# Attention of a streaming Conformer encoder: scores kept negated with a minimum, probabilities scaled by ScalarE, two score tiles of block 0 in one pair of banks

## The chip, the cores and the metric

The kernel runs on one core of a Trainium2 chip. The metric is the device time of one execution in microseconds, the median of several runs. Times within the execution are read from the profile of a single execution, counted from the start of its span. The engines are TensorE (PE in the profile; PEld is its weight load), VectorE (DVE), ScalarE (ACT), GpSimd (POOL) and SyncE (SP, which here issues nearly all DMAs, in order).

## The reference

One layer of a hybrid streaming encoder is computed in fp32 for a prompt of 2048 tokens and a sample chunk of 64 tokens, with model width 1024: a norm, one input projection into the parts of a convolution branch, q, k, v and two gates, then the convolution and the attention, a gated merge with an output projection, and a gated feed-forward part. The attention is over a band: 8 heads of 64 channels, where each chunk of 64 tokens reads its own chunk and the eight before it, with a bias by relative distance.

```python
    s = jnp.einsum('bqhd,bkhd->bhqk', q, k).astype(jnp.float32) * ATTN_SCALE
    rel = jnp.clip(q_pos[:, None] - k_pos[None, :], -MAX_REL, MAX_REL) + MAX_REL
    s = s + rel_bias[:, rel].astype(jnp.float32)[None]
    ...
    p = jax.nn.softmax(s, axis=-1).astype(v.dtype)
    return jnp.einsum('bhqk,bkhd->bqhd', p, v)
```

The attention is computed for the prompt's tokens and for the sample chunk, which reads 256 cached keys and its own 64.

## The kernel before, in words

Products of the big matrices are done in fp32 by pairs of a high and a low part (`whi`, `wlo`, `hh`, `hl`), three matmuls to a product, with their sums (`ps`) in PSUM. The first phase ends at about 1225 us of the profiled execution. It goes through the tokens in four blocks (0 to 576 with the sample chunk, then three of 512); the code numbers them 0 to 3, and the short name of the change calls block 0 block one. For each block the columns of the input projection are done in a fixed order of stages, q, k, v, gates and the two halves of the convolution's input. The norm of the next block's x tiles, the attention, the convolution's 31 taps (`y<-u,wd,y` on DVE, one instruction of 512 or 606 columns for each tap) and the output stages are generators that go alongside these products. They are called lanes. The class `Stream` keeps a modelled load for each engine, adds to it for every instruction, and pumps a lane on when the time or the room that it yielded is reached (`SCORE_ROOM`: DVE at most 2500 ns ahead of PE; `PE_LAG` is 400 ns). So the order of all instructions is fixed when the kernel is built, by these modelled loads and by the framework's own scheduler, and a changed instruction can move others far from it.

Attention works on heads, in block 0 alternately a prompt head and a sample head. A prompt head of block 0 has four score tiles of 128 tokens with 128, 256, 384 and 512 keys, a sample head one tile of 64 x 320, and a head of blocks 1 to 3 four tiles of 128 x 640, kept as twice 320 columns in two banks: 136 tiles in all. `attend` (L1397) writes a tile's scores with `pe.matmul` into `sc`, a pair of PSUM banks of which there is only one (pool `ps_a`, tag "s"), so that the next scores wait until the score pass has read the last. For each tile `softmax_max` (L1299) runs the score pass on DVE (`CUSTOM_DVE_ANT_0 pr<-sc,bias` in the profile, with a read of its accumulator behind it; `ISA pr,sm<-sc,bias` in the order of instructions): it scales scores plus bias into `pr` in SBUF and leaves the row's maximum in `sm`. DVE then negates the maximum (`TENSOR_SCALAR sm<-sm`), ACT takes the exponential with it as bias, and sums the row. `softmax_scale` takes the reciprocal of the sum on DVE and scales the probabilities, on DVE (`TENSOR_SCALAR pr<-pr,sm`) in blocks 0 to 2 and on ACT in block 3 (`ON_ACT`, L48). It is called for a tile after the next tile's scores. PE then transposes the probabilities (`ptp<-ident,pr`), ACT and DVE split them (`ph`, `pl`), and PE multiplies them with v (`po`).

In the profile nearly all engine instructions have one line, L104, that of a helper which records each operation; SP's loads have their own: L1085 x tiles (`x_t`), L1328 and L1329 q and k of a head, L1335 and L1337 its v, L486 stores and L456 loads of split weights, L1260 stores of the convolution's rows (`c_d`). In the changed kernel these lines are one or two off (L103, L1084, L1326, and so on).

Of the kernel before, what the change touches and what calls it, by code (L numbers as in the profile page):

```python
# [8 lines left out]
F32 = mybir.dt.float32  # L9
F32R = mybir.dt.float32r  # L10
AF = mybir.ActivationFunctionType
ALU = mybir.AluOpType
# [4 lines left out]
P = 128  # L17
# [26 lines left out]
PE_LAG = 400.0  # L44
# [3 lines left out]
ON_ACT = (3,)  # L48
# [9 lines left out]
SCORE_ROOM = {"dve": 2500}  # L58
# [530 lines left out]
def streaming_layer(ctx: ExitStack, tc: tile.TileContext, I, O):  # L589
    nc = tc.nc  # L590
    stream = Stream()
# [594 lines left out]

    def convolve(u, y, ct, b):
        w = UW if b == 0 else HIST + QB
        n = w - HIST
# [109 lines left out]
    def softmax_max(ps, n, w, bias):  # L1299
        pr = wk.tile([P, 640], F32, tag="pr", name="pr", bufs=8)  # L1300
        sm = wk.tile([P, 4], F32, tag="sm", name="sm", bufs=9)
        nb = ps.shape[1]
        stream.after("dve", "pe")
        dve.tensor_tensor_reduce(
            out=pr[:n, :w].rearrange("p (a b) -> p a b", a=nb), in0=ps, in1=bias.rearrange("p (a b) -> p a b", a=nb),
            scale=0.125, scalar=-3e38, op0=ALU.add, op1=ALU.max, accum_out=sm[:n, 0:1],
        )
        dve.tensor_scalar(sm[:n, 1:2], sm[:n, 0:1], -1.0, None, ALU.mult)
        free = stream.when("dve")
        stream.after("act", "dve")  # L1310
        act.activation(pr[:n, :w], pr[:n, :w], AF.Exp, bias=sm[:n, 1:2], accum_out=sm[:n, 2:3])
        return pr, sm, free, stream.when("act")

    def softmax_scale(pr, sm, n, w, on_act):
        dve.reciprocal(sm[:n, 3:4], sm[:n, 2:3])
        if on_act:
            stream.after("act", "dve")
            act.activation(pr[:n, :w], pr[:n, :w], AF.Copy, scale=sm[:n, 3:4])
        else:
            dve.tensor_scalar(pr[:n, :w], pr[:n, :w], sm[:n, 3:4], None, ALU.mult)  # L1320
# [57 lines left out]
    order, loaded, now = [], {}, {"scored": -1, "finished": -1, "bias": None}  # L1378
# [21 lines left out]
    def attend(i):  # L1400
# [8 lines left out]
        for t in range(0, nq, P):  # L1409
            n = min(P, nq - t)  # L1410
            ps = ps_a.tile([P, 2, 512], F32, tag="s", name="sc")
# [12 lines left out]
            if t + P < nq:  # L1424
                yield free + PE_LAG, SCORE_ROOM
            else:
                fetch(i + 1)
                now["scored"] = i
            if t:
                softmax_scale(*tiles[-2], x in ON_ACT)  # L1430
        yield ready
        softmax_scale(*tiles[-1], x in ON_ACT)
        yield stream.when("act" if x in ON_ACT else "dve") + PE_LAG
# [680 lines left out]
```

## Time and profile before

| | before |
|---|---|
| time, median of 3 runs (lowest to highest) | 3046.8 us (3046.7 to 3047.27) |
| the profiled execution | 3042.59 us |
| its span | 3040.8 us |
| mean granted clock of PE | 0.986 |
| PE busy | 2934.8 us, 97% of the span |
| DVE busy | 2052.4 us, 67% |
| ACT busy | 1256.8 us, 41% |
| POOL busy | 985.3 us, 32% |

Busy time is the time in which an engine ran at least one instruction. The granted clock is the share of TensorE's full rate that the throttle let through. A row of the timeline has a start, a length, the engine, the operation with its tiles (out<-in), and in brackets how long the engine had been idle before it and whose work ended that. Where a row says x6, it holds six instructions in succession.

### The profile page before, as it was taken

How to read it: one execution, taken by the hardware profiler on the slowest of the kernel's cores; microseconds unless marked ns; L12 is line 12 of the kernel's file. 1: busy time of each engine (PE TensorE's matmuls, PEld its weight loads, DVE VectorE, ACT ScalarE, POOL GpSimd, SP SyncE). 2: the span in 40 equal slices, each digit the busy share in tenths (PEclk: the TensorE clock that was granted, in tenths of full speed). 3: DMA queues.
4: the chain of work that ended last, by engine and by line, in shares of the span. 5: the costliest groups of instructions: out<-in, count | busy, mean ns of one | idle time of the engine just before them, and what ended most of it. 6: DMA issues, size and time to landing. Idle time of an engine off the chain costs nothing. (4 is left out here: it accounts for less than half of the span.)

```text
span 3040.8 us, 44889 instructions
## 1 busy us (share of the span) xinstructions
PE 2934.8 (97%) x16259; PEld 2606.5 (86%) x16259; DVE 2052.4 (67%) x3835; ACT 1256.8 (41%) x2267; POOL 985.3 (32%) x617
## 2 busy tenths in 40 slices
PE   7989898999999999989999999999999999999998
PEld 4889776888888788878989889999999898999997
DVE  5896678777977895467666755655666756366567
ACT  3324532453254257464444425534444244333332
POOL 1200120101011102355677433247767341333331
PEclk9999998999999999999999999999999999999999
DMA  9888788888997788886444786455556965355554
GB/s 305 268 275 299 230 286 278 275 263 268 305 284 243 247 265 282 253 285 215 149 143 144 231 290 207 157 165 190 182 194 201 342 215 190 118 167 173 166 160 176
DMA packets 487019, 690.98 MB, mean 227 GB/s; under 512 B 38420, under 2 KB 316808, under 8 KB 486797
## 3 DMA queue, kind: packets, MB, share of 16 engines
q1 hardware_dynamic: 474517, 670.72, 67.3%
q10 hardware_dynamic: 12280, 17.39, 1.6%
q8 instruction: 128, 2.10, 0.3%
q14 instruction: 94, 0.77, 0.1%
HBM read 503.79 MB, written 184.19 MB: 226 GB/s over the span
## 5 line engine op out<-in xcount | busy, mean ns | idle before, releaser
L104 POOL TENSOR_TENSOR wlo<-wst,whi 128x1024 fp32r<-128x1024 f32 (+1 forms) x180 | 401.4, 2236 | 491.6 <-ACT whi L104 463.9
L104 PE MATMUL ps<-t,whi 128*128 128x384 f32 (+1 forms) x2112 | 506.1, 324 | 10.0 <-DVE t L104 4.8
L104 PE MATMUL pd<-whi,hid 128*128 128x512 f32 (+1 forms) x1400 | 450.2, 391 | 3.4 <-DVE acc L104 3.4
L104 ACT ACTIVATE whi<-wst 128x1024 fp32r<-128x1024 f32 (+1 forms) x273 | 266.1, 979 | 358.6 <-PE ps L104 123.7
L104 PE MATMUL ps<-b,whi 128*128 128x384 f32 (+1 forms) x1584 | 381.7, 326 | 11.0 <-DVE pw L104 4.0
L104 PEld LDWEIGHTS ps<-t,whi 128*128 128x128 f32 x2112 | 370.7, 189 | 18.4 <-DVE t L104 5.9
L104 DVE SCALAR_TENSOR_TENSOR y<-u,wd,y 128x512 f32<-128x512 f32 (+1 forms) x480 | 369.3, 772 | 6.7
L104 PE MATMUL ps<-hh,whi 128*128 128x512 f32 (+2 forms) x992 | 364.6, 367 | 0.7 <-DVE h L104 0.7
L104 PE MATMUL ps<-hl,whi 128*128 128x512 f32 (+2 forms) x992 | 348.1, 351 | 0.0
L104 PE MATMUL ps<-hh,wlo 128*128 128x512 f32 (+2 forms) x992 | 347.6, 350 | 0.0
L104 DVE TENSOR_TENSOR acc<-acc,pd 128x512 f32<-128x512 f32 (+1 forms) x440 | 290.7, 684 | 80.5 <-PE pd L104 76.9
L104 PE MATMUL ps<-t,wlo 128*128 128x384 f32 (+1 forms) x1056 | 340.8, 323 | 0.0
L104 PEld LDWEIGHTS pd<-whi,hid 128*128 128x128 f32 (+1 forms) x1400 | 258.1, 184 | 64.7 <-DVE acc L104 6.9
L104 PEld LDWEIGHTS ps<-b,whi 128*128 128x128 f32 x1584 | 278.7, 190 | 14.3 <-DVE pw L104 4.3
L104 PE MATMUL pd<-wlo,hid 128*128 128x512 f32 (+1 forms) x700 | 273.7, 391 | 0.0
L104 PE MATMUL ps<-b,wlo 128*128 128x384 f32 (+1 forms) x792 | 257.3, 325 | 0.0
L104 POOL TENSOR_TENSOR r<-t,mhalf 128x8 f32<-128x8 f32 (+3 forms) x68 | 84.4, 1243 | 390.0 <-DVE t L104 380.1
L104 PEld LDWEIGHTS ps<-hh,wlo 128*128 128x128 f32 x992 | 188.6, 190 | 22.7
L104 POOL TENSOR_TENSOR wlo<-wup,whi 128x1024 fp32r<-128x1024 f32 (+1 forms) x64 | 138.2, 2160 | 213.0 <-ACT whi L104 190.7
L104 PEld LDWEIGHTS ps<-hh,whi 128*128 128x128 f32 x992 | 189.3, 191 | 19.7 <-issue 1.9
L104 PEld LDWEIGHTS ps<-hl,whi 128*128 128x128 f32 x992 | 189.3, 191 | 15.5 <-issue 1.4
L104 PEld LDWEIGHTS ps<-t,wlo 128*128 128x128 f32 x1056 | 199.3, 189 | 0.6
(217 smaller groups left out, 5717.5 us busy)
## 6 DMA issues: line engine op xcount, KB each, us to landing
whi<-w_din_h SPq DMA_DIRECT2D x72, 512.0 KB, 5.8
wlo<-w_din_l SPq DMA_DIRECT2D x72, 512.0 KB, 7.0
wst<-sum_d SPq DMA_DIRECT2D x131, 256.0 KB, 2.9
wmod<-in_w_ada SPq DMA_DIRECT2D x48, 512.0 KB, 6.7
sum_d<-ws SPq DMA_DIRECT2D x88, 256.0 KB, 3.2
wst<-in_w_ffn_in SPq DMA_DIRECT2D x85, 256.0 KB, 3.4
wst<-in_w_in SPq DMA_DIRECT2D x40, 512.0 KB, 7.1
wst<-in_w_ffn_in SPq DMA_DIRECT2D x37, 512.0 KB, 5.3
```

What stands on the lines that cost most here:

```text
L104: return f(*args, **kw)
```

## The change

The score pass multiplies by −0.125 and keeps a minimum, so that `pr` holds the negated scores and `sm` the negated maximum; the exponential takes it as bias with scale −1, and the negate on DVE goes. All probabilities are scaled on ACT. In block 0 the tiles of 128 and 256 keys are written into the two halves of one pair of banks, those of 384 and 512 into those of the next, and after the first of such two tiles the lane asks only for room, not for the modelled time at which the score pass frees the bank. The dictionary `now` is set up earlier and is given the score pass's instruction, which is not read.

```diff
@@ -45,7 +45,6 @@
 TURN_LAG = 2500.0
 KN_LAG = 5000.0
 X_LAG = 8000.0
-ON_ACT = (3,)
 ON_POOL = ()
 DMA_LAG = 4000.0
 OUT_LAG = 4000.0
@@ -1183,6 +1182,8 @@
                     )
         W.done()
         return u
+
+    now = {"scored": -1, "finished": -1, "bias": None}
 
     def convolve(u, y, ct, b):
         w = UW if b == 0 else HIST + QB
@@ -1298,26 +1299,23 @@
 
     def softmax_max(ps, n, w, bias):
         pr = wk.tile([P, 640], F32, tag="pr", name="pr", bufs=8)
-        sm = wk.tile([P, 4], F32, tag="sm", name="sm", bufs=9)
+        sm = wk.tile([P, 3], F32, tag="sm", name="sm", bufs=9)
         nb = ps.shape[1]
         stream.after("dve", "pe")
-        dve.tensor_tensor_reduce(
+        now["least"] = dve.tensor_tensor_reduce(
             out=pr[:n, :w].rearrange("p (a b) -> p a b", a=nb), in0=ps, in1=bias.rearrange("p (a b) -> p a b", a=nb),
-            scale=0.125, scalar=-3e38, op0=ALU.add, op1=ALU.max, accum_out=sm[:n, 0:1],
+            scale=-0.125, scalar=3e38, op0=ALU.add, op1=ALU.min, accum_out=sm[:n, 0:1],
         )
-        dve.tensor_scalar(sm[:n, 1:2], sm[:n, 0:1], -1.0, None, ALU.mult)
         free = stream.when("dve")
         stream.after("act", "dve")
-        act.activation(pr[:n, :w], pr[:n, :w], AF.Exp, bias=sm[:n, 1:2], accum_out=sm[:n, 2:3])
+        act.activation(pr[:n, :w], pr[:n, :w], AF.Exp, bias=sm[:n, 0:1], scale=-1.0, accum_out=sm[:n, 1:2])
         return pr, sm, free, stream.when("act")
 
-    def softmax_scale(pr, sm, n, w, on_act):
-        dve.reciprocal(sm[:n, 3:4], sm[:n, 2:3])
-        if on_act:
-            stream.after("act", "dve")
-            act.activation(pr[:n, :w], pr[:n, :w], AF.Copy, scale=sm[:n, 3:4])
-        else:
-            dve.tensor_scalar(pr[:n, :w], pr[:n, :w], sm[:n, 3:4], None, ALU.mult)
+    def softmax_scale(pr, sm, n, w):
+        stream.after("dve", "act")
+        dve.reciprocal(sm[:n, 2:3], sm[:n, 1:2])
+        stream.after("act", "dve")
+        act.activation(pr[:n, :w], pr[:n, :w], AF.Copy, scale=sm[:n, 2:3])
 
     def load_qk(h, q0, nq, k0, nk):
         hp, i = divmod(h, 2)
@@ -1375,7 +1373,7 @@
             )
         return bias
 
-    order, loaded, now = [], {}, {"scored": -1, "finished": -1, "bias": None}
+    order, loaded = [], {}
 
     def attention(b):
 
@@ -1408,7 +1406,9 @@
         tiles = []
         for t in range(0, nq, P):
             n = min(P, nq - t)
-            ps = ps_a.tile([P, 2, 512], F32, tag="s", name="sc")
+            if x != 0 or t % (2 * P) == 0:
+                both = ps_a.tile([P, 2, 512], F32, tag="s", name="sc")
+            ps = both if x != 0 or t % (2 * P) == 0 else both[:, 1:]
             if x not in (0, "s"):
                 for j in range(2):
                     for d in range(2):
@@ -1421,16 +1421,18 @@
                 src, bs = ps[:n, 0:1, :w], bias[:n, 64:384][:, ::-1] if x == "s" else bias[:, :w][:, ::-1]
             pr, sm, free, ready = softmax_max(src, n, w, bs)
             tiles.append((pr, sm, n, w))
-            if t + P < nq:
+            if x == 0 and t % (2 * P) == 0:
+                yield stream.load["pe"], SCORE_ROOM
+            elif t + P < nq:
                 yield free + PE_LAG, SCORE_ROOM
             else:
                 fetch(i + 1)
                 now["scored"] = i
             if t:
-                softmax_scale(*tiles[-2], x in ON_ACT)
+                softmax_scale(*tiles[-2])
         yield ready
-        softmax_scale(*tiles[-1], x in ON_ACT)
-        yield stream.when("act" if x in ON_ACT else "dve") + PE_LAG
+        softmax_scale(*tiles[-1])
+        yield stream.when("act") + PE_LAG
         while now["finished"] < i - 1:
             yield lambda: now["finished"] == i - 1
         fetch_v(i + 1)
```

By the orders of instructions of both kernels DVE loses 136 `TENSOR_SCALAR sm<-sm` and 104 `TENSOR_SCALAR pr<-pr,sm` (8 of each narrow width and 64 of 128 x 640), ACT gains 104 scales, and PE, POOL and SP have the same instructions as before in another order. The orders first differ at about 184 us of the profiled execution and are the same again from the end of the first phase. Three places follow.

The first prompt head of block 0, on PE. `ps` are products of the convolution's input stage, `q_1737` is the head's q. Before:

```order
L104 MATMUL ps<-hh,wlo 128x288
L104 MATMUL sc<-kk,q_1737 128x128 x2
L104 MATMUL sc<-kk,q_1737 128x256 x2
L104 MATMUL sc<-kk,q_1737 128x384 x2
L104 MATMUL sc<-kk,q_1737 128x512 x2
L104 MATMUL ptp<-ident,pr 128x128 x6
L104 MATMUL ps<-hh,whi 128x288
L104 MATMUL ps<-hl,whi 128x288
```

After:

```order
L103 MATMUL ps<-hh,wlo 128x288
L103 MATMUL sc<-kk,q_1737 128x128 x2
L103 MATMUL sc<-kk,q_1737 128x256 x2
L103 MATMUL sc<-kk,q_1737 128x384 x2
L103 MATMUL ptp<-ident,pr 128x128
L103 MATMUL sc<-kk,q_1737 128x512 x2
L103 MATMUL ptp<-ident,pr 128x128 x2
L103 MATMUL ps<-hh,whi 128x288
L103 MATMUL ps<-hl,whi 128x288
L103 MATMUL ps<-hh,wlo 128x288
L103 MATMUL ps<-hh,whi 128x288
```

The scores stand 25 rows earlier on PE, the products that were ahead of them come behind, and the first transpose stands between the third score and the fourth. On DVE seven taps of the convolution stand ahead of the head's first score pass, as before.

The loads of two x tiles, on SP, near 346 us. `c_d` are stores of convolution rows, `w_din` and `w_dqkv` split weights. Before, with the six loads of a sample head (q, k and v) a few rows ahead:

```order
L1260 DMA c_d<-part_h 128x64
L1260 DMA c_d<-part_l 128x64
L456 DMA whi<-w_din_h 128x1024
L456 DMA wlo<-w_din_l 128x1024
L1085 DMA x_t<-in_x_prompt 128x1024
L382 DMA wst<-in_w_conv_out 128x4x128
L382 DMA wst<-in_w_attn_out 128x4x128
L486 DMA w_dqkv_3_h<-whi 128x1024
L486 DMA w_dqkv_3_l<-wlo 128x1024
L1085 DMA x_t<-in_x_prompt 128x1024
L1328 DMA q_3947<-q_d 64x2x512
L1329 DMA kk<-k_d 64x512
```

After:

```order
L1261 DMA c_d<-part_h 128x64
L1261 DMA c_d<-part_l 128x64
L1333 DMA vv<-v_d 128x4x128
L1084 DMA x_t<-in_x_prompt 128x1024
L455 DMA whi<-w_din_h 128x1024
L455 DMA wlo<-w_din_l 128x1024
L1084 DMA x_t<-in_x_prompt 128x1024
L1326 DMA q_3977<-q_d 64x2x64
L1327 DMA kk<-k_d 64x320
L1326 DMA q_3977<-q_d 64x2x64
L1327 DMA kk<-k_d 64x320
L381 DMA wst<-in_w_conv_out 128x4x128
```

The two loads stand closer together, with two weight loads between them instead of four other transfers besides; the loads of the next head's q and k come behind them. The first of the two is the SP's 247th row before and its 252nd after. On PE the transposes of the first of these tiles stand at row 1760 before and 1764 after, with a head's four transposes and its first two products with v ahead of them; those of the second tile, before in two halves at rows 1780 and 1792, all stand at row 1793.

The end of block 0 and the start of block 1. The last sample head on PE, with q in `q_5057` before:

```order
L104 MATMUL ps<-wlo,hh 128x512
L104 MATMUL sc<-kk,q_5057 64x320 x2
L104 MATMUL ps<-whi,hl 128x512
L104 MATMUL ptp<-ident,pr 128x64 x2
L104 MATMUL ptp<-ident,pr 64x64
L104 MATMUL ps<-hh,whi 128x512
L104 MATMUL ps<-hl,whi 128x512
```

After, where the scores `sc<-kk,q_4935` stand seven rows ahead of the first row shown, after the product `ps<-whi,hh`:

```order
L103 MATMUL ps<-wlo,hh 128x512
L103 MATMUL ps<-whi,hl 128x512
L103 MATMUL ps<-whi,hh 128x512
L103 MATMUL ps<-wlo,hh 128x512
L103 MATMUL ps<-whi,hl 128x512
L103 MATMUL ps<-whi,hh 128x512
L103 MATMUL ps<-wlo,hh 128x512
L103 MATMUL ps<-whi,hl 128x512
L103 MATMUL ptp<-ident,pr 128x64 x2
L103 MATMUL ptp<-ident,pr 64x64
L103 MATMUL ps<-whi,hh 128x512
```

One product stood between the scores and the first transpose, and now 14 do. At the seventh prompt head, a little earlier, the scores of 128 and of 256 keys stand at PE's rows 1981 and 1986 before and at 1798 and 1916 after, and those of 384 and 512 at 1936 and 1944.

The first head of block 1, on DVE (`A_173` belongs to a norm's modulation, `y` are taps). Before:

```order
L104 TENSOR_TENSOR A_173<-pa,cols 128x2x2x2
L104 SCALAR_TENSOR_TENSOR y<-u,wd,y 128x512
L104 TENSOR_TENSOR A_173<-A_173,cols 128x2x2x2
L104 SCALAR_TENSOR_TENSOR y<-u,wd,y 128x512 x12
L104 ISA pr,sm<-sc,bias 128x640
L104 ISA sm 128x1
L104 SCALAR_TENSOR_TENSOR y<-u,wd,y 128x512
L104 TENSOR_SCALAR sm<-sm 128x1
L104 SCALAR_TENSOR_TENSOR y<-u,wd,y 128x512
L104 ISA pr,sm<-sc,bias 128x640
L104 ISA sm 128x1
```

After:

```order
L103 TENSOR_TENSOR A_173<-pa,cols 128x2x2x2
L103 SCALAR_TENSOR_TENSOR y<-u,wd,y 128x512
L103 TENSOR_TENSOR A_173<-A_173,cols 128x2x2x2
L103 SCALAR_TENSOR_TENSOR y<-u,wd,y 128x512 x15
L103 ISA pr,sm<-sc,bias 128x640
L103 ISA sm 128x1
L103 SCALAR_TENSOR_TENSOR y<-u,wd,y 128x512 x2
L103 ISA pr,sm<-sc,bias 128x640
L103 ISA sm 128x1
L103 RECIPROCAL sm<-sm 128x1
L103 SCALAR_TENSOR_TENSOR y<-u,wd,y 128x512
L103 ISA pr,sm<-sc,bias 128x640
```

Fifteen taps instead of twelve stand ahead of the first score pass, and the negates and scales are gone from between. On PE all four scores of this head now stand ahead of its first transposes; before it was three.

## The prediction, made before the run

> **What bounds the kernel now.** I read the page's busy table, the clock line and the chain first.
>
> ```profile
> span 3040.8 us, 44889 instructions
> PE   7989898999999999989999999999999999999998
> PEclk9999998999999999999999999999999999999999
> PE 40%; DVE 1%; DMA 1%; issue 0%; ACT 0%; POOL 0%; SPq 0%; DVEq 0%; POOLq 0%; ACTq 0%
> ```
>
> TensorE (PE) is the bound: nearly every slice is full, and the chain of work that ended last names almost nobody else. The 136 score tiles take VectorE (DVE) time off a busy engine, but that can pay only where PE stands still for it. The code after the first phase is in the same order in both kernels, so I look between 184 us, the first row that differs, and 1225 us, by the table of stretches (columns: window, length, busy PE, PEld, DVE, ACT, POOL with counts, then granted clock, DMA share, GB/s).
>
> ```profile
> 184.00:206.00 22.00, 13.81 (x68) 11.56 (x67) 19.68 (x44) 5.40 (x14) 0.00 (x0) 0.69 0.96 310
> 206.00:262.00 56.00, 54.92 (x402) 52.99 (x401) 53.27 (x109) 22.13 (x50) 1.78 (x3) 1.00 0.80 256
> 346.00:372.00 26.00, 17.50 (x69) 12.51 (x68) 13.56 (x42) 10.57 (x25) 6.87 (x6) 0.74 0.69 199
> 420.00:437.00 17.00, 13.13 (x55) 9.99 (x54) 12.74 (x36) 5.93 (x15) 2.06 (x1) 0.80 0.39 118
> 475.00:489.00 14.00, 10.66 (x38) 7.95 (x37) 8.88 (x20) 2.10 (x7) 1.24 (x2) 0.76 1.01 385
> 503.00:521.00 18.00, 9.07 (x39) 7.31 (x38) 16.86 (x35) 3.41 (x8) 0.00 (x0) 0.72 0.31 110
> 521.00:1000.00 479.00, 475.41 (x2654) 399.24 (x2653) 376.97 (x798) 201.32 (x386) 58.18 (x52) 1.00 0.85 270
> 1050.00:1225.00 175.00, 173.99 (x917) 146.63 (x915) 129.94 (x276) 106.96 (x186) 22.38 (x16) 1.00 0.87 273
> ```
>
> PE stands still at five places and nowhere else to speak of: 479 us of blocks one to three show 475.41 us of PE. At each place the clock is low as well. I price a place as idle time plus (1 − clock) × window: 8.2 + 6.8 = 15.0 us for the first head of block 0; 8.5 + 6.8 = 15.3 at 346 to 372; 3.9 + 3.4 = 7.3 at the seventh head (420); 3.3 + 3.4 = 6.7 at the last sample head (475); 8.9 + 5.0 = 14.0 at the first head of block 1 (503). Together 58 us: that is all there is to win. The table of PE's waits from 187 to 520 us says who ends them (total, times, longest):
>
> ```profile
> PE sc L104 <- DVE sm L104: 19.6, 7, 8.0
> PE ptp L104 <- DVE pr L104: 5.0, 4, 3.3
> PE ps L104 <- ACT hh L104: 4.8, 1, 4.8
> PE pt L104 <- DVE x_t L104: 3.5, 1, 3.5
> ```
>
> 19.6 us are scores (sc) waiting for the bank that the score pass on DVE frees; 5.0 transposes (ptp) waiting for scaled probabilities; 8.3 the norm of x tiles.
>
> **The change, part by part.** First the work, by groups (count, then total and mean ns):
>
> ```profile
> L104 ACT ACTIVATE pr<-pr,sm 128x640 f32<-128x640 f32 x128 | 104.6, 827 | 104.2 <-DVE sm L104 102.9 <-ACT gate L104 0.8
> L104 ACT ACTIVATION_READ_ACCUMULATOR pr<-pr,sm 128x1 f32 x128 | 23.9, 187 | 0.0
> L104 DVE CUSTOM_DVE_ANT_0 pr<-sc,bias 128x640 f32<-128x640 f32 x96 | 78.6, 819 | 26.2 <-PE sc L104 23.2 <-DMA bias<-rb_d 1.1 <-PE ptp L104 1.0
> L104 DVE TENSOR_SCALAR pr<-pr,sm 128x640 f32<-128x640 f32 x64 | 38.1, 595 | 0.8
> L104 DVE TENSOR_SCALAR sm<-sm 128x1 f32<-128x1 f32 x128 | 18.9, 148 | 1.0
> L104 DVE SCALAR_TENSOR_TENSOR y<-u,wd,y 128x512 f32<-128x512 f32 x360 | 268.4, 748 | 4.8
> L104 DVE SCALAR_TENSOR_TENSOR y<-u,wd,y 128x606 f32<-128x606 f32 x120 | 100.9, 844 | 1.9
> ```
>
> DVE loses 136 negates (18.9 us for 128 of them) and 104 scales (38.1 us for the 64 of 640 columns; the 40 narrower ones are under that each). The score pass with a minimum I cost as it is with a maximum: same operands, bounds nothing either way. ScalarE (ACT) gains 104 scales, 64 of them at the 827 ns of the same form, 53 us. Per tile the path from score to transpose loses a negate (0.15) and gains 0.83 − 0.60 = 0.23 us for the slower scale: nearly nothing. It is 0.82 + 0.08 + 0.83 + 0.19 + 0.16 + 0.83, about 2.9 us of work, and 3.9 with the conv taps between. In blocks 1 to 3 the changed order leaves at least 4.1 us of products between a score and its first transpose, except at block 1's first head, so there I cost it at nothing; block 3 scales on ACT already, and its window 1050 to 1225 shows 1.0 us idle in 175. If that cover failed, each of 64 tiles would cost the 0.23 us of its slower scale, 15 us in all.
>
> The Trainium skill, "Perfetto Trace Analysis", section Optimizing Scalar/DVE Operations, speaks against half of it: where DVE has a performance mode it is the faster engine, and moving work off it makes sense if it is saturated. The rows agree on the first (595 against 827 ns); by the second, the scales would be moved for nothing in 521 to 1000, where DVE is busy 377 of 479 us, and rightly at the first head, 19.68 of 22.
>
> So what counts is the order at each place.
>
> **First head.** DVE has conv taps ahead of the first score pass:
>
> ```profile
> 187.89 5.26 DVE L104 SCALAR_TENSOR_TENSOR y<-u,wd,y 128x606 f32<-128x606 f32 x6
> 193.41 0.79 PE L104 MATMUL sc<-kk,q 128*128 128x256 f32 x2 [5.59 <-DVE sm L104]
> 187.09 0.29 PE L104 MATMUL ps<-hh,whi 128*128 128x288 f32 x1
> 187.22 0.29 PE L104 MATMUL ps<-hl,whi 128*128 128x288 f32 x1
> ```
>
> The taps stay ahead. PE now reaches the scores 25 products earlier, 25 × 0.13 = 3.3 us more of waiting; one pair of banks lets it write two scores, but the third waits for both passes. The 25 products come behind it and cover part of the wait for the scaled probabilities. I take **+3 us**, bounds 0 (all won back) and +6 (none, and a slower clock for longer). Of the third head, whose tiles now have 31, 23 and 17 products, 4.2, 3.1 and 2.3 us, before their transposes against the path's 3.9, the second and third lack 0.8 and 1.6: **+2.5**, bounds 0 and +5.
>
> **The x tiles at 346.**
>
> ```profile
> 346.04 0.42 SPq L1085 DMA_DIRECT2D x_t<-in_x_prompt  x1
> 348.91 0.65 SPq L1085 DMA_DIRECT2D x_t<-in_x_prompt  x1
> 355.92 0.69 PE L104 MATMUL pt<-ident,x_t 128*128 128x128 f32 x2 [3.51 <-DVE x_t L104]
> 359.71 0.63 ACT L104 ACTIVATE junk<-x_t 128x512 f32<-128x512 f32 x1 [4.88 <-DMA x_t<-in_x_prompt]
> ```
>
> The two loads were issued with four stores and weight loads between and a sample head's six loads ahead; now two stand between, and that head's q and k come after. SP reaches the first of them about five issues later, some 1 to 3 us at 0.4 to 0.65 us each; but PE comes to the transposes later too, behind a whole head's four transposes and its first products with v, and to the second tile behind 24 products (24 × 0.23 = 5.5 us) that before were split around its two halves. The load then has about 4 us more to land and the second, in the old order 10.8 us from issue to use, is asked for sooner. I take most of it as gone, **−12**, bounds −15 and 0 (the DMA is what paces it).
>
> **Seventh head.**
>
> ```profile
> 420.07 0.39 PE L104 MATMUL ps<-wlo,hh 128*128 128x512 f32 x1
> 420.30 0.40 PE L104 MATMUL ps<-whi,hl 128*128 128x512 f32 x1
> 425.96 0.50 PE L104 MATMUL sc<-kk,q 128*128 128x256 f32 x2 [3.21 <-DVE sm L104]
> ```
>
> The second score waited with four products since the first; now there are some 110 between, and it needs no bank from the first. What is left is the third, 20 rows later. **−5.5**, bounds −7.3 and 0. The Trainium skill, "TensorE: Matmul & The Clock Gate", section on the HAM clock gate, says that the array falls to half rate after an idle window of about 3.4 us and comes back after about as much work. An estimate from it is 3.4 / 2 = 1.7 us per trip; this window shows 0.20 × 17 = 3.4 us behind waits of 3.21 and some tenths, twice that. By the page, four such trips at the three places won are worth 7 us and not the 13.6 that the windows show, and the sum would be about −5 instead of −12; the measured clock decides.
>
> **Last sample head.**
>
> ```profile
> 476.66 0.46 PE L104 MATMUL sc<-kk,q 128*64 128x320 f32 x2
> 478.75 0.56 ACT L104 ACTIVATE pr<-pr,sm 64x320 f32<-64x320 f32 x1 [5.99 <-DVE sm L104]
> 480.69 0.36 PE L104 MATMUL ptp<-ident,pr 64*128 64x64 f32 x3 [3.33 <-DVE pr L104]
> ```
>
> From score to transpose are 4.0 us with one product between; now 14 products, 14 × 0.23 = 3.2 us, stand there. Under a microsecond is left and the clock need not drop: **−6**, bounds −6.7 and 0.
>
> **First head of block 1.**
>
> ```profile
> 502.77 9.41 DVE L104 SCALAR_TENSOR_TENSOR y<-u,wd,y 128x512 f32<-128x512 f32 x12
> 512.98 1.43 PE L104 MATMUL sc<-kk,q 128*128 128x320 f32 x4 [8.00 <-DVE sm L104]
> ```
>
> Twelve taps stand ahead of its first score pass, and now fifteen: 3 × 0.78 = 2.3 us more of wait. All four scores stand ahead of the first transposes, so the third pass (0.82 and a tap, 1.6 us) is waited for barely covered, and the scale is 0.23 us slower for each of four tiles: **+5**, bounds 0 and +8.
>
> Small new waits at heads whose tiles come closer: **+1**, bounds −2 and +4. Sum: 3 + 2.5 − 12 − 5.5 − 6 + 5 + 1 = −12.0.
>
> **The rivals.** *(a) The x tiles still wait.* At 346 the page has PE waiting for a load; if SP's queue gives it its place by what landed before, five more issues ahead put it as late as PE. For: 10.8 us from issue to use. Against: 4 us more of PE's work ahead. The sum is then 0: 3042.6, a median of 3046.8. *(b) The pair of banks only hands the wait on.* The seventh head's third score waits for two passes where the second waited for one: −5.5 falls away, −6.5 in all, 3040.3. For: the same taps are on DVE. Against: 20 rows, 4.6 us of products, between. *(c) Slower: ACT's queue is in order.* A tile's scale now stands behind the next tile's exp and its read, 0.83 + 0.19, and lasts 0.23 longer, so the probabilities come 1.2 us later at the heads where tiles follow one another closely, six of them by the changed order (the first and third, three sample heads, block 1's first). If that makes a wait long enough to drop the clock as at 420, 3.4 us each, it is 20 us; −12 becomes +8, some 3055 as a median. It decides from a delay of one to two microseconds at each. For: the scale is not hidden where only two microseconds of products stand. Against: block 3, 1.0 idle of 175. *(d)* That the change does less than it says is excluded: the negates and scales are gone from DVE's order.
>
> **How the numbers follow.** The profiled execution took 3042.6 us (its span 3040.8), 4.2 under the median of 3046.8, so the forecast is 3030.6 for a profiled execution, 3034.8 as a median. Its own range is 3025 (the x tiles and the last sample head won wholly, the new waits half as long) to 3040. Chances: forecast 0.50, (a) 0.16, (b) 0.10, (c) 0.24. A measurement of this kernel can tell some 0.2%, 6 us, from no change: faster is 0.50 and half of (b), 0.55; within it (a) and the other half, 0.21; slower 0.24. The range, 3025 to 3056, leaves out the far part of (c) and a little below.
>
> **What would show it.** Right: at the seventh head and the last sample head no PE wait above a microsecond and a full clock; the x tile's transposes waiting under 2 us; the first head of block 1 with a wait of about 10 us; DVE 70 us less busy and ACT 75 more with PE's time unchanged; nothing different after 1225 us but its start. Wrong: a wait of ptp for pr released by ACT at many tiles (rival c), pt still behind x_t (a), or the third score of a head waiting 3 us (b).

## The result and the profile after

The changed kernel took 3040.08 us (median of 18 runs, 3032.76 to 3047.91), the kernel before 3046.75 us (18 runs, 3040.81 to 3050.88). The ratio is 0.9982, 95% interval 0.9975 to 0.9989: 5.5 us less (3.4 to 7.6), where 12 were forecast. The profiled execution shown here is one of the longer of the 18, 3045.71 us with a span of 3043.9; how that can be with a faster kernel is said below. One execution of e2, the one that was profiled, took 3240.66 us at a granted clock of 0.843 and is left out of its ratio.

The page's head, busy table and chain after:

```profile
span 3043.9 us, 44749 instructions
PE 2932.8 (96%) x16259; PEld 2609.7 (86%) x16259; DVE 1996.2 (66%) x3595; ACT 1321.8 (43%) x2371; POOL 984.2 (32%) x617
PE 40%; DVE 2%; DMA 1%; issue 1%; ACT 0%; SPq 0%; POOL 0%; DVEq 0%; ACTq 0%; POOLq 0%
```

VectorE is 56 us less busy and ScalarE 65 more, and PE's busy time is the same within 2 us: the change does what it says, and PE is still the chain. The forecast of 70 and 75 us was of the rows' own times, and these sum to 76 less and 75 more; rows overlap in part, and busy time counts an overlap once. The groups of 640 columns, by count, total and mean ns:

```profile
L103 ACT ACTIVATE pr<-pr,sm 128x640 f32<-128x640 f32 x192 | 156.2, 826 | 89.1 <-DVE sm L103 87.8 <-ACT gate L103 0.4
L103 DVE CUSTOM_DVE_ANT_0 pr<-sc,bias 128x640 f32<-128x640 f32 x96 | 78.6, 818 | 32.7 <-PE sc L103 31.4 <-DMA bias<-rb_d 0.5
```

The 64 more scales cost 826 ns each, and a score pass with a minimum costs 818 ns, as with a maximum. The stretches shown of before, after (same columns), with three added, since heads have moved: the seventh prompt head's scores are now written from 376 to 414, the last sample head's at 461, and block 1's first head begins at 494.

```profile
184.00:206.00 22.00, 13.70 (x67) 11.24 (x66) 19.62 (x39) 6.54 (x19) 0.00 (x0) 0.69 0.56 157
346.00:372.00 26.00, 18.27 (x68) 13.11 (x68) 11.81 (x33) 12.34 (x27) 4.98 (x5) 0.80 0.95 287
372.00:420.00 48.00, 46.17 (x250) 36.84 (x248) 39.05 (x84) 23.08 (x46) 11.88 (x9) 1.00 0.80 267
420.00:437.00 17.00, 15.61 (x81) 12.63 (x81) 15.33 (x32) 8.17 (x20) 5.09 (x3) 1.00 0.70 184
437.00:475.00 38.00, 37.41 (x204) 29.85 (x205) 32.31 (x66) 13.55 (x32) 0.75 (x2) 1.00 0.94 331
475.00:489.00 14.00, 14.00 (x83) 10.13 (x82) 4.50 (x9) 0.60 (x1) 1.45 (x3) 1.00 1.03 377
489.00:503.00 14.00, 5.43 (x28) 4.40 (x26) 13.47 (x20) 0.60 (x1) 0.00 (x0) 0.77 1.06 350
503.00:521.00 18.00, 14.54 (x63) 11.78 (x64) 14.49 (x29) 9.28 (x17) 1.39 (x2) 0.71 0.58 150
521.00:1000.00 479.00, 471.32 (x2617) 395.53 (x2616) 334.58 (x663) 241.43 (x440) 50.82 (x50) 1.00 0.83 266
1050.00:1225.00 175.00, 171.19 (x908) 145.39 (x906) 127.76 (x243) 108.34 (x187) 22.63 (x16) 1.00 0.87 272
```

The clock is full from 372 to 489, the seventh head and the last sample head within it; the x tiles' place is nearly as it was; the hole of block 1's first head has grown and come earlier; and blocks 1 to 3, which had 3.6 us of idle PE in 521 to 1000, have 7.7. PE's waits of 187 to 520 us after:

```profile
PE sc L103 <- DVE sm L103: 19.5, 8, 10.2
PE pt L103 <- DVE x_t L103: 3.9, 2, 3.6
PE ps L103 <- ACT hh L103: 3.4, 2, 2.3
PE ptp L103 <- ACT pr L103: 1.7, 3, 0.7
```

The scores wait as long for their bank as before, 19.5 us against 19.6, but half of it is now one wait of 10.2. The transposes' 5.0 us are 1.7.

**A table by PE's work.** Orders differ, so the same clock time is not the same place in two kernels. For every PE row I took the PE work that stands ahead of it (rows by their mean cadence outside waits and the low clock) and subtracted it from the start that the trace gives. The growth of the difference between two points of PE's work is what PE lost there, idle time and low clock together. "Start" is when the last PE row begins that all kernels have in the same place. The last point is the start of a row near the end of the first phase, at 1196.5 us before and 1194.3 after, from which on PE's order is the same again. The sum is free of cadences, since the same rows lie between these two; a place is to be read by its difference from another kernel's, as the cadences leave some constant us in each column. In us, with the experiments told of below:

```
                             start  first  heads    x    7th   last  block1   to     lost in
kernel                       (at)   head   2 to 5 tiles  head  head  1st    the same all from
                                    146-   180-   285-  330-  365-   head     row    the start
                                    180    285    330   365   410   410-430 430-1073  on
before                      184.1   13.4    4.7   16.6   7.6   9.9   13.8    19.0     85.0
changed                     186.0   13.1    3.9   14.9   3.8   3.9   18.0    23.1     80.8
changed again (e5)          184.6   13.5    4.0   14.2   5.7   3.9   18.6    23.1     83.0
no pair (e1)                185.9   12.2    9.2   15.0   4.1  11.0   11.7    24.1     87.4
scales on VectorE (e6)      186.3   12.3    3.2   13.7   2.8   3.9   15.8    27.2     78.9
x tiles early (e3)          185.0   13.5    4.1   10.3   9.1   4.0   19.1    26.3     86.4
block 1's taps held (e4)    187.1   13.3    4.1   15.2   8.3  13.4   11.2    25.0     90.4
pair alone (e7)             185.3   15.8    6.5   15.0  16.1   2.5    9.6    16.0     81.5
ScalarE alone (e8)          185.9   12.9    3.8   22.5   2.5   9.7    7.4    24.2     83.0
one tile's taps held (e9)   184.3   13.8    4.2   14.0   3.2   9.7   15.1    20.8     80.8
e9, scales on VectorE (e10) 185.6   12.3    3.1   14.0   2.5  10.0   13.3    24.2     79.4
e10 and x early (e11)       185.0   13.8    4.5   10.3   6.0  10.1   13.1    25.9     83.8
minimum, model's line (e12) 185.1   12.3    0.3   23.9   3.5   3.7   15.4    18.7     77.7
```

Two executions of the changed kernel agree within 2 us in every place, so a place can be read from one profile to about that. With the same order, the start goes from 184.1 to 187.1 us. From the last point of the table to PE's last row, with the same order, the execution before took 1836.2 us and the changed kernel's 1841.5. So the changed kernel's profiled execution began this part 1.9 us late, won 4.2 in it and lost 5.3 after it. That is how a faster kernel has a longer span here, and why verdicts below are made from the timed ratios, and causes from this table.

**A line of the change that is none of its three parts.** `softmax_scale` has a new `stream.after("dve", "act")` ahead of the reciprocal. It adds no instruction; it raises the modelled load of VectorE to at least that of ScalarE, and by this it moves the order. It is in the changed kernel, in e1 to e6 and in e9 to e12, and not in the kernel before, e7 and e8. No run has it alone, or takes it alone away. By the orders that the kernels build to it moves much: ahead of block 1's first score pass the changed kernel would have 4 taps in a row instead of 15 without it, e12 6 instead of 11, and e8 15 instead of 4 with it.

### The profile page after: what moved, and what is told of

It is laid out like the page before. It is cut to its first block, busy times and chain, and to the rows that moved or that the text cites. A ratio compares the mean times of both kernels' runs of the same rounds, so it can differ in the third digit from the quotient of the medians.

```text
span 3043.9 us, 44749 instructions
## 1 busy us (share of the span) xinstructions
PE 2932.8 (96%) x16259; PEld 2609.7 (86%) x16259; DVE 1996.2 (66%) x3595; ACT 1321.8 (43%) x2371; POOL 984.2 (32%) x617
## 5 line engine op out<-in xcount | busy, mean ns | idle before, releaser
L103 PEld LDWEIGHTS ps<-b,whi 128*128 128x128 f32 x1584 | 277.9, 189 | 14.9 <-DVE pw L103 4.3
L103 ACT ACTIVATE pr<-pr,sm 128x640 f32<-128x640 f32 (+3 forms) x272 | 200.1, 747 | 128.1 <-DVE sm L103 126.2
L103 POOL TENSOR_TENSOR r<-t,mhalf 128x1 f32<-128x1 f32 (+3 forms) x68 | 82.2, 1211 | 412.8 <-DVE t L103 369.1
```

The lines of the kernel that those rows point to most:

```text
L103: return f(*args, **kw)
```

## The experiments

Each was timed against the kernel before on the same chip, in 33 to 35 runs of the latter and 11 or 12 of its own.

**e1, no pair of banks**

```diff
-            if x != 0 or t % (2 * P) == 0:
-                both = ps_a.tile([P, 2, 512], F32, tag="s", name="sc")
-            ps = both if x != 0 or t % (2 * P) == 0 else both[:, 1:]
+            ps = ps_a.tile([P, 2, 512], F32, tag="s", name="sc")
...
-            if x == 0 and t % (2 * P) == 0:
-                yield stream.load["pe"], SCORE_ROOM
-            elif t + P < nq:
+            if t + P < nq:
```

> The changed kernel without its third part: each score tile of block 0 has a pair of banks of its own again; minimum and ScalarE scaling stay. Theory: the gain is made of places whose order moved, and the pair of banks is what gave it at the first head and the seventh. In this order the seventh head has 10 product rows (2.5 us) between first and second score, so its wait comes back only in part (2 to 4 us of the 5.9 won), the first head goes back to before's order (+2), but only 6 taps instead of 15 stand ahead of block 1's first score pass, -6 to -7 us there. Sum: 3 to -2 us against the changed kernel, 3038 to 3043. Rival A, the pair is the source of the whole gain: 3046 or more. Rival B, the pair of banks costs (it holds two scores back for one): 3034 or less, with gains at block 0's heads and not only at block 1's first.

Measured: 1.0004 of the kernel before (0.9994 to 1.0015). The gain is gone, so rival A's number came out, but not as it or I had it: the seventh head kept what it had won (it loses 4.1 us), block 1's first head won 6 as forecast, and heads 2 to 5 lost 5.3 and the last sample head 7.1, the latter with a wait of transposes for ScalarE, which itself had waited 3.90 us for VectorE's score pass:

```profile
477.54 0.58 PE L103 MATMUL ptp<-ident,pr 64*128 64x64 f32 x3 [5.73 <-ACT pr L103]
```

**e2 and e6, blocks 0 to 2 scaled on VectorE again**

```diff
-        stream.after("act", "dve")
-        act.activation(pr[:n, :w], pr[:n, :w], AF.Copy, scale=sm[:n, 2:3])
+        if on_act:
+            stream.after("act", "dve")
+            act.activation(pr[:n, :w], pr[:n, :w], AF.Copy, scale=sm[:n, 2:3])
+        else:
+            dve.tensor_scalar(pr[:n, :w], pr[:n, :w], sm[:n, 2:3], None, ALU.mult)
...
```

Here `on_act` is a new parameter, true in block 3 alone.

> The changed kernel with the probabilities of blocks 0 to 2 scaled on VectorE again (ScalarE in block 3, as before); minimum and pair of banks stay. Its order is nearly that of the changed kernel up to block 1, with 14 taps instead of 15 ahead of block 1's first score pass. Theory: which engine scales is worth nothing by itself; within 3 us of the changed kernel (3037 to 3043), the first heads of blocks 0 and 1 still wait 5 and about 9 us, PE idle in blocks 1 and 2 (521 to 1000 us) changes by under 3 us. Rival, ScalarE's in-order queue gives back what the rest wins: 5 us or more faster than the changed kernel (3035 or less), and the idle 7.7 us of 521 to 1000 goes back to the 3.6 of before.

> The same kernel as in e2 (blocks 0 to 2 scaled on VectorE, minimum and pair kept), on the same chip as the changed kernel and with a profile that can be read by stages. Theory 1, scaling on ScalarE costs nothing: within 2 us of the changed kernel, and blocks 1 to 3 after their first head lose about 20 us like it (before: 15). Theory 2, ScalarE's scaling is what gives 5 us back there: these blocks lose 15 to 17 us, and the kernel is 3 us or more faster than the changed one.

Measured: 0.9972 (0.9963 to 0.9982) in e2, 0.9977 (0.9967 to 0.9987) in e6; the stages are read from e6, the same kernel. These are the lowest ratios of all kernels tried. Against the changed kernel beside it (e5, 0.9990) it is about 0.1%, some 4 us, which both intervals together hardly resolve. Theory 2 of e6 falls: blocks 1 to 3 lose 27.2 us here, not less than with ScalarE's scaling (23.1). What is better stands in block 0 and at block 1's first head (15.8 against 18.0).

**e3, x tiles early**

```diff
-        x_t = load_x(t, P, wa, "x", 3)
+        x_t = early.pop(t) if t in early else load_x(t, P, wa, "x", 3)
         yield stream.load["pe"] + X_LAG
         r = square(x_t, P)
+        if lo == PBLOCKS[1][0] and t < lo + 2 * P:
+            early[t + 2 * P] = load_x(t + 2 * P, P, wa, "x", 3)
```

> The changed kernel with the loads of the third and fourth x tile of block 1 issued right after the squares of the first and second, at SP's rows 239 and 240 instead of 252 and 255; PE's order stays nearly the same. Theory: at 346 to 372 the change let PE come 4 us later, but SP came to the load 5.2 us later too (351.25 against 346.04), so nothing was won there; 13 rows earlier are 8 us or more, the wait of the transposes for x_t (3.6) and of the products for hh (2.3) go with the low clock: 8 to 12 us faster than the changed kernel, 3028 to 3032. Rival, the DMA engines are full and the loads land no sooner, or push the v and k loads behind them: within 3 us, 3037 to 3043, with PE waiting for other loads there.

Measured: 0.9995 (0.9986 to 1.0003), so not faster than the changed kernel at all. First the changed kernel's rows at the place, then those of e3 (SPq rows are SP's issues):

```profile
351.25 0.50 SPq L1084 DMA_DIRECT2D x_t<-in_x_prompt  x1
353.10 0.70 SPq L1084 DMA_DIRECT2D x_t<-in_x_prompt  x1
360.04 1.33 PE L103 MATMUL pt<-ident,x_t 128*128 128x128 f32 x5 [3.61 <-DVE x_t L103]
365.62 0.79 PE L103 MATMUL ps<-whi,hh 128*128 128x512 f32 x1 [2.33 <-ACT hh L103]
```

```profile
339.50 0.92 SPq L1084 DMA_DIRECT2D x_t<-in_x_prompt  x2
353.83 1.04 PE L103 MATMUL pt<-ident,x_t 128*128 128x128 f32 x8
358.94 0.80 PE L103 MATMUL ps<-whi,hh 128*128 128x512 f32 x1 [4.08 <-ACT hh L103]
433.45 0.66 PE L103 MATMUL sc<-kk,q 128*128 128x128 f32 x2 [1.20 <-DMA kk<-k_d]
```

In e3 both loads are issued 12 us sooner, and the transposes do not wait for x_t. So the load was what came last there. But the products behind them then wait 4.08 us for `hh`, which VectorE and ScalarE make from the transposes: the place loses 10.3 us instead of 14.9, where 8 to 12 us less were expected. And the eighth prompt head's scores, whose loads stand in the same queue, come 1.2 us late for a load of k, with 6.83 us at half rate from 433.4 on: 330 to 365 loses 9.1 instead of 3.8 to 5.7. The theory is right on the cause, half right on the size, and the gain is not kept.

**e4, block 1's taps held**

```diff
-            yield
+            yield lambda: b != 1 or now["scored"] >= 16
```

> The changed kernel with block 1's convolution taps held back until the first head of block 1 has its scores issued; in the order 12 taps instead of 20 then stand on VectorE between the convolution's input and the first score pass. Theory: the 10.2 us wait for that score pass is taps and nothing else; 8 x 0.78 = 6.2 us shorter, and the low clock shorter by some: 6 to 9 us faster than the changed kernel, 3031 to 3034. Rival, something else releases it (the modulation's row on VectorE, the load of k, ScalarE): the wait stays over 8 us, or another place gives it back, within 3 us of the changed kernel.

Measured: 1.0016 (1.0006 to 1.0026), slower than before. At block 1's first head it did what it should (11.2 us instead of 18.0; the wait 4.0 instead of 10.2). But the order changed in block 0 too: at the eighth head the next convolution tile's input, its first tap and three more now stand ahead of the first score pass on VectorE, where in the changed kernel no tap of that tile does. The second score waited 3.84 us for this pass, with 10.24 us at half rate, and the column 365 to 410 loses 13.4 us instead of 3.9.

```profile
450.32 0.69 DVE L103 SCALAR_TENSOR_TENSOR u<-tb,ps 128x512 f32<-128x512 f32 x1 [5.42 <-PE ps L103]
451.63 2.33 DVE L103 SCALAR_TENSOR_TENSOR y<-u,wd,y 128x512 f32<-128x512 f32 x3
453.87 0.28 DVE L103 CUSTOM_DVE_ANT_0 pr<-sc,bias 128x128 f32<-128x128 f32 x1
454.22 0.79 PE L103 MATMUL sc<-kk,q 128*128 128x256 f32 x2 [3.84 <-DVE sm L103]
```

**e5, the changed kernel again**

> The changed kernel itself again, so that it stands on the same chip and against the same runs of the kernel before as the next three. All theories: 0.998 of the kernel before within 0.1%. Its profile tells how much the stages wander from execution to execution: by the theory that the order fixes the waits, first head 11 to 12 us, x tiles 14, the heads between them and block 1 about 5, block 1's first head 17 to 18, blocks 1 to 3 after that 20 us; by chance, each would move by more than 3 us.

Measured: 0.9990 (0.9981 to 0.9998), again faster than before, by 3 us; with the first 0.9982 the change is worth 3 to 6 us. The stages repeat (table).

**e7, the pair of banks alone**, put into the kernel before (the diff of e1, the other way):

> The kernel before with the pair of banks alone. In its order 7 taps instead of 12 stand ahead of block 1's first score pass (wait 8.0 - 5 x 0.78 = 4.1 us), the seventh head has 62 rows between first and second score, and nothing is changed in the work of VectorE and ScalarE. Theory (the gain comes from the order at block 0's heads, and the pair is enough for it): 8 us or more faster than before, 0.997, blocks 1 to 3 losing 15 us. Rival (the gain needs VectorE relieved of negates and scales): within 3 us of before, with new waits of sc for sm at block 0's heads.

Measured: 0.9997 (0.9988 to 1.0006). Block 1's first head is better by 4.2 us (7 taps instead of 12), the blocks after it lose the least of all, 16.0; yet it is given back at one place in block 0, where a sample head's transposes wait for probabilities that VectorE scales behind taps:

```profile
PE sc L104 <- DVE sm L104: 16.5, 11, 4.8
PE ptp L104 <- DVE pr L104: 12.2, 4, 9.2
PE sc L104 <- DMA kk<-k_d: 7.1, 4, 2.8
```

These are its waits from 187 to 530 us: one of 9.2 us alone, with 13.65 us at half rate from 430.4 on, within and behind it.

**e8, ScalarE's scaling alone** (without the model's new line)

```diff
-ON_ACT = (3,)
+ON_ACT = (0, 1, 2, 3, "s")
```

> The kernel before with all probabilities scaled on ScalarE and nothing else. In its order 4 taps instead of 12 stand ahead of block 1's first score pass (wait 8.0 - 8 x 0.78 = 1.8 us), the seventh head has 140 rows between first and second score. If ScalarE's scaling gives back 5 us in blocks 1 to 3 (theory 2 of e6), these lose 20 us here and the kernel is 2 to 8 us faster than before by its block 0 and block 1's first head. If it costs nothing (theory 1), they lose 15 and it is 8 to 15 us faster.

Measured: 1.0006 (0.9997 to 1.0016): neither theory's gain. The seventh head and block 1's first head won 5 and 6 us on the kernel before, the x tiles lost 6 and blocks 1 to 3 five. The 4 taps at block 1's first head are there only without the model's line, so that gain is not what ScalarE's scaling brings within the change.

**e9, one convolution tile's taps held**

```diff
-            yield
+            yield lambda: b != 1 or ct != 1 or now["scored"] >= 16
```

> The changed kernel with the taps of block 1's second convolution tile alone held until the first head of block 1 has its scores issued (e4 held all of block 1's taps, and so changed block 0's heads too). Order and waits up to there are those of the changed kernel; 11 taps instead of 15 stand in one row ahead of the first score pass. Theory: the wait is taps, 4 x 0.78 = 3.1 us plus some of the low clock; that place loses 13.5 to 15 us instead of 18, block 0 the same as the changed kernel within 2 us, and the kernel is 3 to 4 us faster than the changed one if nothing is given back. Rival: what is won there is given back in blocks 1 to 3, which lose 23 us or more instead of 20.

Measured: 0.9991 (0.9982 to 1.0001), the same as the changed kernel. The wait is 3.15 us shorter for four taps fewer:

```profile
495.44 8.63 DVE L103 SCALAR_TENSOR_TENSOR y<-u,wd,y 128x512 f32<-128x512 f32 x11
504.87 1.43 PE L103 MATMUL sc<-kk,q 128*128 128x320 f32 x4 [7.03 <-DVE sm L103]
```

but the last sample head lost 5.8 us, twice what the place won. No product stands between its scores and its transposes here, 14 in the changed kernel; the same holds for e1, e10 and e11, and all four lose 9.7 to 11.0 us there instead of 3.9. Blocks 1 to 3 gave nothing back (20.8).

**e10 and e11, combinations:** the hold of e9 with VectorE's scaling, and this with the x tiles early.

> The same hold with blocks 0 to 2 scaled on VectorE (minimum and pair kept), 11 taps instead of e6's 14. Theory: 2 to 3 us faster than e6, 0.9967 of the kernel before; block 1's first head loses 13 us instead of 15.5. Rival (given back behind): 0.9977 as e6.

> The kernel of e10 with the third and fourth x tile of block 1 loaded early, at SP's rows 232 and 236 instead of 252 and 255. Theory: as in e3 the place of the x tiles loses 4 us less or more (10 instead of 14); whether it is kept depends on the loads of k behind it. Kept: 0.995 to 0.996. Given back to k's loads, as in e3: 0.997 to 0.998.

Measured: 0.9992 (0.9983 to 1.0001) and 1.0002 (0.9992 to 1.0011), neither better than e6 without either edit: e11 is clearly slower, e10 by its ratio, though its interval overlaps e6's. In e10 the first head of block 1 won 2.5 us against e6 and the last sample head lost 6.1. In e11 the x tiles won 3.7 us against e10; 330 to 365 lost 3.5, the heads ahead of the x tiles 2.9 and blocks 1 to 3 1.7.

**e12, the minimum and the model's line**: the new score pass and no negate, VectorE's scaling in blocks 0 to 2, no pair (the diffs of e1 and e2 together on the changed kernel). The expectation calls it the minimum alone, but the model's new line is still in it.

> The kernel before with the minimum alone: no negate, scaling on VectorE in blocks 0 to 2, no pair of banks. In its order 9 taps, one product of the convolution's input and 11 more taps stand ahead of block 1's first score pass, and the seventh head has 13 rows between its first and second score. Theory (the give-back in blocks 1 to 3 comes with any lighter VectorE, whichever instruction is taken away): these lose about 20 us, against 15 before and 12 with the pair alone. Rival (it comes from ScalarE's scaling or from the pair): 15 us. In all between 0.997 and 1.001 of the kernel before.

Measured: 0.9980 (0.9971 to 0.9989): the minimum with the model's line brings as much as the whole change; what the minimum brings alone is not shown. Blocks 1 to 3 lose 18.7 us, as before, so the theory that any lighter VectorE gives back there falls. So does the rival: e6 has nothing but the pair more than e12 and loses 27.2 there, and e7 has the pair and loses 16.0.

**Taps against the wait.** Over the kernels, the wait of the second score at block 1's first head goes with the number of taps in a row right ahead of the first score pass:

```
taps in the row     4     6     7     7    11    11    11    12    14    15    16
wait, us          1.68  3.27  3.67  4.00  6.16  7.03  7.18  8.00  9.59 10.18 10.95
kernel             e8    e1    e7    e4   e10    e9   e11  before e6  changed e3
```

From 4 to 15 taps it grows by 8.5 us (to the changed kernel's 10.18), 0.77 a tap, and 15 of them take 11.78 us, 0.79 each. What releases this wait is shown: it is the score pass behind its taps. (In e12 a row of the convolution's input splits the taps, and it is left out.)

## Why the prediction came out, point by point

The sign was right and the time lies in the range; the size is less than half of what was forecast: −12 forecast, −5.5 measured (−3.0 in the repeat). The range of 3025 to 3056 reaches from 22 us below the kernel before to 9 above it, and so holds the numbers of all the rivals. The measured 3040.1 is also the number of rival (b), 3040.3, whose mechanism did not come: that is luck. The table's sum for the profiled execution, 80.8 against 85.0, is −4.2 (−2.0 in the repeat). Two of the places came out as forecast and by their mechanism (the last sample head and block 1's first head), the seventh head in part, and the x tiles hardly at all; that the sum is not nearer to nothing is owed to the first heads, which cost nothing where 5.5 us were forecast.

- **What bounds the kernel** holds: PE is the chain, and the five places priced at 58 us together lose 61 by the table (13.4 + 16.6 + 7.6 + 9.9 + 13.8), constant part included.
- **The work** holds: per tile nearly nothing, the scale at 826 ns, the minimum at 818.
- **First head: +3 forecast, −0.3 measured** (+0.1 in the repeat). Of the 3.3 us of waiting that I added ahead only 1.9 appeared, and that partly for another reason:

```profile
188.43 0.41 PE L103 MATMUL sc<-kk,q 128*128 128x128 f32 x2 [2.10 <-DMA kk<-k_d]
194.21 0.80 PE L103 MATMUL sc<-kk,q 128*128 128x256 f32 x2 [5.37 <-DVE sm L103]
```

2.10 us for the load of k and 5.37 for the score pass stand against 5.59 before. The other step that failed is that the 25 products "cover part": twelve of them stand between the third transpose and the next, where PE had nothing but the probabilities to wait for, and the waits of transposes there, 1.4 us before, are gone, so that PE's idle time in 184 to 206 is 8.3 us against 8.2. The third head's +2.5 did not come either: heads 2 to 5 together lose 0.8 us less. My path of 3.9 us is that of 640 columns; an exponential of 256 takes 504 ns, not 826.
- **x tiles: −12 forecast, −1.7 measured** (−2.4). This is the step that failed, and the largest error of the sum. PE did come later, as I had it: its wait for the transposes began at 356.4 instead of 352.4. But SP came to the first load at 351.25 instead of 346.04, 5.2 us later, where I had put 1 to 3. I counted five more issues at 0.4 to 0.65 us; in the changed kernel six of the stores and loads just ahead take 0.9 to 1.6 us each. By e3 the load is the cause; by e3 also, the most that an earlier load got there was 4.6 us, since the wait for `hh` is next, and I had taken nothing as late next. The prediction's own sign of being wrong, transposes still behind `x_t` by 2 us or more, came (3.61 us). Rival (a) names this mechanism; its sum, nothing won, failed since the first heads did not cost the 5.5 us that it too counts.
- **Seventh head: −5.5 forecast, −3.8 measured** (−1.9; the repeat has one low stretch of 3.41 us at 436). No score of that head waits for a bank there now. Rival (b), a wait of the third score, did not come in the changed kernel. The pair is not what did it, though: without the pair (e1) the place loses 4.1, with ScalarE's scaling alone (e8) 2.5, and with the pair alone (e7) 16.1. It is the order that each of them happens to bring.
- **Last sample head: −6 forecast, −6.0 measured** (−6.0): its wait of 3.33 and the low clock are gone, and 437 to 489 is at full clock. The products in between go with it over the kernels: with 0 to 2 of them (before, e1, e8 to e11) that place loses 9.7 to 11.0 us, with 12 to 53 (the others) 2.5 to 4.0, but for e4, where the eighth head's wait lies in the same column.
- **Block 1's first head: +5 forecast, +4.2 measured** (+4.8), by the mechanism that the table of taps shows. The changed kernel's rows:

```profile
492.04 11.78 DVE L103 SCALAR_TENSOR_TENSOR y<-u,wd,y 128x512 f32<-128x512 f32 x15
504.61 1.43 PE L103 MATMUL sc<-kk,q 128*128 128x320 f32 x4 [10.18 <-DVE sm L103]
```

10.18 against the "about 10 us" forecast; the later passes cost somewhat less than I had allowed. That there are fifteen taps is owed to the model's line, by the orders told above: without it there would be 4.
- **Small new waits: +1 forecast, +4.1 measured** (+4.1), at the upper bound. They are in blocks 1 to 3, where I had costed the change at nothing because probabilities have 4 us of cover. They do: no transposes wait there. What waits is something else, after:

```profile
PE sc L103 <- DMA kk<-k_d: 3.7, 3, 1.8
PE pa L103 <- DVE R L103: 2.4, 1, 2.4
PE ps L103 <- ACT hh L103: 1.9, 3, 1.1
```

The loads of k, a row of the modulation, and the norm's `hh`; of before, the largest wait in 521 to 1225 was one load of a weight, 2.8 us. For one of them the trace shows ScalarE's queue: at 668.07 an exponential and a scale of 128 x 640 run 1.54 us ahead of the copy to `hh`, and PE waits 1.13 us for it.

```profile
668.07 1.54 ACT L103 ACTIVATE pr<-pr,sm 128x640 f32<-128x640 f32 x2
669.51 0.62 ACT L103 ACTIVATE hh<-h 128x512 fp32r<-128x512 f32 x1
670.18 0.51 PE L103 MATMUL ps<-whi,hh 128*128 128x512 f32 x1 [1.13 <-ACT hh L103]
```

So rival (c) has its place, though not at the tight heads, where ptp waits 1.7 us in all for ScalarE, at most 0.7 at once. As the whole of the 4.1 us it falls by e6, which scales blocks 1 and 2 on VectorE and loses more there. Why these blocks lose 16 to 19 us in the kernel before, with the pair alone and in e12, and 21 to 27 in the others, stays open: no single part goes with it.

The clock: the 10.2 us wait in the changed kernel goes with 17.07 us at half rate, the 3.84 us wait in e4 with 10.24. The Trainium skill, "TensorE: Matmul & The Clock Gate", section on the HAM clock gate, has the array back at full rate after a busy window of about 3.4 us; an estimate from this is 1.7 us for a trip. The low stretches in the first phase come in multiples of 3.41 us, which agrees, and last one to five of them, so that the windows' price, not the minimum, was the one to use: the stretches that went at the seventh and the last sample head had lasted 6.83 us each. That the sum by that estimate, about −5, lies near the result is luck, since it still counts more than 8 us for the x tiles, where 1.7 came.

## What to carry to other kernels

In a kernel whose order is built by modelled loads, taking 56 us of busy time from an engine that is not the bound buys only what the new order buys. Here the minimum with the model's line brings −6 us, the pair alone and ScalarE's scaling alone nothing that their intervals resolve (−1 and +2), and all together −3 to −6; no place's gain can be added to another's. A line that only changes the model is a part of the change like the others, and wants a run of its own, which is missing here. Price each place by what it waits for and by what is late next, and give the places that you did not look at a term of their own size: two fifths of what the seventh head and the last sample head won here (4.1 of 9.8 us) was lost in stretches that looked full. Before a local fix is kept, time it whole: five that shortened the wait that they were made for (e3, e4, e9, e10, e11) gained nothing or lost.

## What the runs showed that was not expected

With the same order up to it, one PE row starts between 184.1 and 187.1 us from one profiled execution to another, and with the same order behind the first phase the rest takes 1835.5 to 1841.5 us; single times of one kernel spread over up to 16 us. A change of 5 us is seen only in ratios of many runs. The minimum costs nothing over the maximum (818 and 819 ns). And one line that adds no instruction, only a modelled load, moves the number of taps at one place from 4 to 15, which by the table of taps is about 8.5 us of wait there; no run has timed it.
